# Output projections of a two-layer streaming encoder: the work on the combined tokens goes into four pieces, each placed in the engine queues behind a given split of weights

## The chip, the cores and the metric

The kernel runs on one core of a Trainium2 chip. The metric is the device time of one execution in microseconds; the median of several executions is compared. The engines go by their names in the profile: PE is TensorE (matrix products), PEld its weight loads, DVE is VectorE, ACT is ScalarE, POOL is GpSimd and SP is SyncE, which here only issues transfers.

## What is computed

The reference is one step of an encoder with two layers, on 512 prompt tokens and 8 x 16 sample tokens, 640 in all. What matters here is the last part of each layer: the outputs of three head groups are concatenated to 2048 features per token, multiplied by the output weights, and added to the residual.

```python
    y = jnp.concatenate([y_a, y_b, y_c], axis=-1) @ w_out
    return x + y, new_conv, new_k, new_v
```

All numbers are float32. The kernel keeps that precision with TensorE's faster format: it splits each operand into a rounded part and the rest, and multiplies three of the four combinations.

## The kernel before

**Layout.** Tokens are the columns: R holds 16 blocks of 128 features (rows of blocks k = 0 to 15) by 640 tokens. HL holds the split of R: blocks 0 to 15 the rounded parts, 16 to 31 the rests. The tokens are halved into TA (0 to 319) and TB (320 to 639), and the 16 feature blocks are cut into KS (0 to 3), KB (4 to 9) and KA (10 to 15).

**Splits.** `split` (line 136) makes the rounded part with one ScalarE activation (line 138) and the rest with one VectorE subtraction (line 139). It is used for tokens and for weights. Both lines therefore show in the profile for many things; the tile names tell them apart: sr is a raw block of output weights, sh its rounded part, sl its rest; th and tl are the two parts of combined tokens in tiles of their own; HL is written for the rest of the tokens.

**Output projection.** `proj` (line 740) multiplies output tiles 0 and 1 of each layer in the plain way: four weight blocks of four feature blocks, each multiplied with both token halves, three products each, so 24 matmuls of 320 columns per weight block (line 749). Tile 0 takes its weights through `wprep`, tile 1 through `s_prep` (line 773), which loads with SP into one of six sr buffers and splits into one of two sh and one of two sl buffers.

The other output tiles come in pairs through `s_pair` (line 818). It saves one of the eight products of a 2 x 2 block product over (output tile, token half) and (KA, KB), in the manner of Winograd and Strassen. a11, a21, a22 and a12 are the raw weights of the two tiles j1, j2 for KA and KB. VectorE makes the sums s1 = a21 + a22, s2 = s1 - a11, and in place a21 = a11 - a21 and a12 = a12 - s2. The products are, in the order of the code for all pairs but the last: a11 with (KA, TA) into X; a12 with (KB, TA) and a12 - s2 with (KB, TB) into z1 (`plain`); the KS columns of tile j1 and of tile j2 (`rest`; the prediction calls their weights r1 and r2); then p7, p6, p4 and p5, which multiply with the combined tokens T3, T2, T4 and T1. Each six-block product is 18 matmuls (line 810).

**Combined tokens.** `combos` (line 783) runs once per layer, after tile 1. It makes sums and differences of the token blocks in place in R (`sub`, line 778), in two groups of three blocks, and splits the results: T2, T3 and T4 into th and tl, T1 into HL over (KA, TB), which nothing else needs any more. That is eight subtractions and eight splits of 128 x 960. In layer 1 the copy y12d keeps R's (KA, TB) for the last two output tiles (line 1063); the second subtraction of a group overwrites what it reads.

**What sets the order.** The framework lays out one queue per engine before the run, from priorities, dependences and its own estimate of times; the engines then work through their queues in that order. Weights are loaded and split under `high_priority`; combos() has ordinary priority. Nothing else fixes where its work stands between the splits of weights. SP's loads are chained in program order (`load`, line 147). The residual tile of each output row is loaded by POOL into R itself (line 823), as soon as that row of R is free; a row of KB is free when T2 and T4 have been split, a row of KA when T3 and T1 have.

`tc.issue_after(ins)` makes every instruction that its block traces on ins's engine stand behind ins in that engine's queue. It is an order of issue and no wait for ins to finish.

Of the kernel before, what the change touches and what calls it, by code (L numbers as in the profile page):

```python
# [58 lines left out]
def build(nc, tc, ctx, A):  # L59
# [23 lines left out]
    def tl(shape, tag, bufs, dt=F32, pl=None):  # L83
        uid[0] += 1
        pl = pl or (cur[home[tag]] if tag in home else sb)
        return pl.tile(shape, dt, tag=tag, name=f"{tag}_{uid[0]}", bufs=bufs)
# [7 lines left out]
    def g2(shape, dt=F32):  # L94
        return tl(shape, "g2", 8, dt)
# [10 lines left out]
    def pa():  # L106
        return tl([P, 512], "a", 4, F32, ap_)

    def pz():
        return tl([P, 2, 512], "z", 2, F32, zp)  # L110
# [4 lines left out]
    R = sb.tile([P, NK, TOK], F32, tag="R", name="R")  # L115
# [8 lines left out]
    ks = Rf[:, (C0 + 3) * TOK + 288:(C0 + 3) * TOK + 288 + P]  # L124
# [8 lines left out]
    def half(t):  # L133
        return t.rearrange("p (s n) -> p s n", s=2)

    def split(raw, scale=None, hi=None, lo=None):
        if scale is None:
            a = ac.activation(hi, raw, AF.Copy)  # L138
            v = ve.tensor_tensor(out=lo, in0=raw, in1=hi.bitcast(F32), op=ALU.subtract)  # L139
        else:  # L140
            a = ac.activation(hi, raw, AF.Copy, scale=scale)
            v = ve.scalar_tensor_tensor(
                out=lo, in0=raw, scalar=scale, in1=hi.bitcast(F32), op0=ALU.mult, op1=ALU.subtract
            )
        return a.ins, v.ins
# [92 lines left out]
    def passes(a, b):  # L238
        return ((a[0], b[0]), (a[0], b[1]), (a[1], b[0]))
# [515 lines left out]
    KS, KB, KA = slice(0, 4), slice(4, 10), slice(10, 16)  # L755
    TA, TB = slice(0, HT), slice(HT, TOK)

    def s_raw(n=6):
        return tl([P, 768], "sr", 6, F32, cur["sw"])[:, :n * P]

    def s_split(raw):
        n = raw.shape[-1]
        hi = tl([P, 768], "sh", 2, F32R, cur["sw"])[:, :n]
        lo = tl([P, 768], "sl", 2, F32R, cur["sw"])[:, :n]
        split(raw, None, hi, lo)
        return hi, lo

    def s_load(src):
        raw = s_raw(src.shape[-1] // P)
        load(raw, src)  # L770
        return raw
# [5 lines left out]
    def sub(out, a, b):  # L777
        ve.tensor_tensor(out=out, in0=a, in1=b, op=ALU.subtract)

    def hl(ks, cs):  # L780
        return HL[:, ks, cs], HL[:, slice(NK + ks.start, NK + ks.stop), cs]

    def combos():
        T = {}
        tt = [
            (tl([P, 6, HT], f"th{n}", 1, F32R, cur["tt"]), tl([P, 6, HT], f"tl{n}", 1, F32R, cur["tt"]))
            for n in (2, 3, 4)
        ]
        T[2], T[3], T[4] = tt
        T[1] = hl(KA, TB)  # L790
        gs = [(slice(KA.start + g, KA.start + g + 3), slice(KB.start + g, KB.start + g + 3)) for g in (0, 3)]
        for a, b in gs:
            sub(R[:, a, TA], R[:, a, TB], R[:, a, TA])
            sub(R[:, a, TB], R[:, b, TB], R[:, a, TB])
            sub(R[:, b, TB], R[:, b, TB], R[:, a, TA])
        place = {1: (0, TA), 2: (1, TB), 3: (0, TB), 4: (1, TA)}
        for n in (3, 2, 4, 1):
            for g, ab in enumerate(gs):
                i, cs = place[n]
                if n == 4:  # L800
                    sub(R[:, ab[1], TA], R[:, ab[1], TA], R[:, ab[1], TB])
                ks = slice(3 * g, 3 * g + 3)
                split(R[:, ab[i], cs], None, T[n][0][:, ks, :], T[n][1][:, ks, :])
        return T

    def s_mm(out, w, x, start, stop):
        n = w[0].shape[-1] // P
        for k in range(n):
            for i, (a, b) in enumerate(passes(w, x)):
                pe.matmul(  # L810
                    out, a[:, k * P:(k + 1) * P], b[:, k, :], start=start and k == 0 and i == 0,
                    stop=stop and k == n - 1 and i == 2, skip_group_check=True,
                )

    def add_to(out, ps):
        ve.tensor_tensor(out=out, in0=ps, in1=out, op=ALU.add)  # L816

    def s_pair(l, j1, T, resid, early=None):
        j2 = j1 + 1
        wj = [A["w_out"][l, j1], A["w_out"][l, j2]]  # L820
        cut = [slice(ks.start * P, ks.stop * P) for ks in (KA, KB, KS)]
        for j in (j1, j2):
            gp.dma_start(R[:, j, :], resid[j])
        X, Dd = pa()[:, :HT], pa()[:, :HT]
        with tc.high_priority():
            a11 = s_load(wj[0][:, cut[0]])
            a21 = s_load(wj[1][:, cut[0]])
            a22 = s_load(wj[1][:, cut[1]])
            a12 = s_load(wj[0][:, cut[1]])
            p1 = s_split(a11)  # L830
            s1, s2 = s_raw(), s_raw()
            ve.tensor_tensor(out=s1, in0=a21, in1=a22, op=ALU.add)
            sub(s2, s1, a11)
            sub(a21, a11, a21)
        s_mm(X, p1, hl(KA, TA), True, True)
        add_to(R[:, j1, TA], X)

        z1 = z2 = None

        def rest(z, j, start, raw=None):  # L840
            with tc.high_priority():
                w = s_split(raw or s_load(wj[j - j1][:, cut[2]]))
            for s, cs in enumerate((TA, TB)):
                s_mm(z[:, s, :HT], w, hl(KS, cs), start, True)

        def plain(start):
            with tc.high_priority():
                w = s_split(a12)
            s_mm(z1[:, 0, :HT], w, hl(KB, TA), start, not start)
            with tc.high_priority():  # L850
                sub(a12, a12, s2)
                w = s_split(a12)
            s_mm(z1[:, 1, :HT], w, hl(KB, TB), start, not start)

        def into(j, z):
            add_to(half(R[:, j, :]), z[:, :, :HT])

        def mixed(raw, n, out, start, dst):
            with tc.high_priority():
                w = s_split(raw)  # L860
            s_mm(out, w, T[n], start, True)
            for j, cs in dst:
                add_to(R[:, j, cs], out)

        p6 = (s2, 2, X, False, [(j2, TA)])
        p7 = (a21, 3, Dd, True, [(j2, TB)])
        p5 = (s1, 1, X, False, [(j2, TB), (j1, TB)])
        p4 = (a22, 4, Dd, False, [(j2, TA)])
        order = (p7, p6, p4, p5)
        if early:  # L870
            for a in order:
                mixed(*a)
            with tc.high_priority():
                st = [s_load(w[:, cut[2]]) for w in wj]
            early(0)
            z1, z2 = pz(), pz()
            rest(z1, j1, True, st[0])
            rest(z2, j2, True, st[1])
            early(1)
            into(j2, z2)  # L880
            plain(False)
            early(2)
            into(j1, z1)
        else:
            z1 = pz()
            plain(True)
            rest(z1, j1, False)
            into(j1, z1)
            z2 = pz()
            rest(z2, j2, True)  # L890
            into(j2, z2)
            for a in order:
                mixed(*a)

    for l in range(L):
# [35 lines left out]
        for n, (kind, i) in enumerate(ZT):  # L931
# [9 lines left out]
            if l == 0 and 2 <= n < 10:  # L941
                for h in (n - 2, n + 6):
                    a = bscr[h:h + 1, :]
# [33 lines left out]
            elif kind in ("k", "v"):  # L977
                raw = g2([P, 512])
# [14 lines left out]
                else:  # L993
# [5 lines left out]
                    for h in range(2):  # L999
                        hi = V[h][:, :, rows2[h]]  # L1000
# [11 lines left out]
            elif kind == "q":  # L1012
                raw = zt()[:, :512]
# [4 lines left out]
                for h in range(2):  # L1018
                    q = qh([P, 512])
                    hi = q[rows2[h]]  # L1020
# [10 lines left out]
            elif kind == "cq":  # L1031
                raw = zt()[:, :512]
# [32 lines left out]
        resid = A["xT"] if l == 0 else x1d  # L1065
        done = NK if l == 0 else NK - 2
        T, W = None, []
# [29 lines left out]
        for j in list(range(2)) + list(range(2, done, 2)):  # L1097
            if j < 2:
                res = zt()
                gp.dma_start(res, resid[j])  # L1100
                ps = proj(
                    [A["w_out"][l, j][:, c * 512:(c + 1) * 512] for c in range(4)], s_prep if j else wprep
                )
                ve.tensor_tensor(out=half(R[:, j, :]), in0=ps[:, :, :HT], in1=half(res), op=ALU.add)
            else:
                s_pair(l, j, T, resid, turn if j + 2 == done else None)
            if j == 0:
                close_pool("wp")
                open_pool("tt", "right")
            if j == 1:  # L1110
                T = combos()
            for i in range(j, j + 1 if j < 2 else j + 2):
                if l == 0:
                    gp.dma_start(x1d[i], R[:, i, :])
                add_sq(i, i == 0, acc)
# [4 lines left out]
    parts = (slice(0, 384), slice(384, TOK))  # L1120
# [168 lines left out]
```

## Time and profile before

| | us |
|---|---|
| median of 3 runs (lowest, highest) | 1848.38 (1848.2, 1850.27) |
| the profiled execution | 1848.52 |
| its span, first to last instruction | 1846.7 |
| around the span | 1.8 |

The granted TensorE clock over the span is 0.997 of full speed. The first tiles of the output projection, with which the change deals, lie at about 764 to 800 us in layer 0 and 1625 to 1658 us in layer 1. The page gives busy times and shares of the span; a timeline gives instructions in order of time, start and length in us, with equal neighbours merged (the length is then that of all of them); a view by windows gives start:end, length, and for PE, PEld, DVE, ACT and POOL the busy time with the count of instructions, then the granted clock, the busy share of the DMA engines and what they moved in GB/s; the view of waits gives total, count and longest; the view of a tile gives shortest, median and longest in ns. The view of DMA issues gives the count, the size and the median time from issue to landing.

### The profile page before, as it was taken

The numbers are of one execution on the slowest core, as the hardware profiler recorded it, in microseconds if no ns is written. First come the engines' busy times: TensorE is split into PE (matmuls) and PEld (weight loads), VectorE is DVE, ScalarE is ACT, GpSimd is POOL, SyncE is SP. The second block draws the span as 40 slices with busy tenths as digits, with TensorE's granted clock in tenths as the row PEclk, the third lists the DMA queues.
The fourth block names the chain that finished last, engine by engine and source line by source line (L and its number), as shares of the span: only waits on it lengthen the run. The fifth ranks groups of instructions, "written<-read, shape, count | busy, mean of one in ns | idle before, by whom it ended". The sixth has DMA issues, their size and how long they took to land.

```text
span 1846.7 us, 32347 instructions
## 1 busy us (share of the span) xinstructions
PE 1817.5 (98%) x12612; PEld 1766.3 (96%) x12612; DVE 1257.8 (68%) x2562; ACT 786.6 (43%) x1609; POOL 160.7 (9%) x351
## 2 busy tenths in 40 slices
PE   8999999999999999999999999999999999999996
PEld 7999999999998999999999999999999899989996
DVE  7959989567555435966686999766655444676765
ACT  7832224556544334533352222555755333533331
POOL 1121210000000010100020000000000010010000
PEclk9999999999999999999999999999999999999998
DMA  8844442222222343543333332222232244452233
GB/s 281 294 122 107 103 127 76 74 63 72 84 81 76 92 158 117 167 135 112 111 98 92 81 86 77 74 68 76 67 87 81 75 132 132 140 175 76 77 113 120
DMA packets 89001, 202.30 MB, mean 110 GB/s; under 512 B 11872, under 2 KB 16912, under 8 KB 88816
## 3 DMA queue, kind: packets, MB, share of 16 engines
q1 hardware_dynamic: 68848, 139.75, 25.3%
q0 software_dynamic: 17536, 57.60, 10.1%
q10 hardware_dynamic: 2464, 2.88, 0.4%
q8 instruction: 99, 1.62, 0.4%
q14 instruction: 54, 0.44, 0.1%
HBM read 184.84 MB, written 20.33 MB: 111 GB/s over the span
## 4 chain that ended last, share of the span: by engine, by line
PE 94%; DVE 3%; DMA 1%; issue 0%; ACT 0%; DVEq 0%; ACTq 0%
PE z L749 59%; PE a L810 9%; PE z L810 9%; PE z L301 2%; PE a L278 2%; PE a L497 2%; PE a L540 2%; PE a L477 2%; PE z L1134 1%; DVE R L1167 1%; PE a L528 1%; DMA wr<-w_in 1%; PE a L636 1%; PE a L675 1%; PE a L662 1%; PE a L571 1%
## 5 line engine op out<-in xcount | busy, mean ns | idle before, releaser
L749 PE MATMUL z<-HL,wh 128*128 128x320 f32 x4992 | 973.8, 312 | 0.0
L749 PEld LDWEIGHTS z<-HL,wh 128*128 128x128 f32 x4992 | 787.8, 188 | 8.9 <-issue 5.6
L749 PE MATMUL z<-HL,wl 128*128 128x320 f32 x2496 | 584.1, 312 | 1.0 <-DVE wl L139 1.0
L749 PEld LDWEIGHTS z<-HL,wl 128*128 128x128 f32 x2496 | 419.6, 188 | 4.5 <-issue 1.6
L138 ACT ACTIVATE wh<-wr 128x512 fp32r<-128x512 f32 x316 | 198.6, 629 | 467.4 <-PE z L749 383.9
L139 DVE TENSOR_TENSOR wl<-wr,wh 128x512 fp32r<-128x512 f32 x316 | 217.7, 689 | 177.8 <-ACT wh L138 165.4
L425 DVE SCALAR_TENSOR_TENSOR R<-R,sm 128x128 f32<-128x128 f32 (+1 forms) x480 | 235.2, 550 | 0.1
L138 ACT ACTIVATE sh<-sr 128x768 fp32r<-128x768 f32 (+1 forms) x125 | 98.2, 788 | 203.3 <-PE z L810 92.4
L810 PE MATMUL z<-HL,sh 128*128 128x320 f32 x728 | 161.1, 309 | 2.9 <-ACT sh L138 2.9
L139 DVE TENSOR_TENSOR sl<-sr,sh 128x768 fp32r<-128x768 f32 (+1 forms) x125 | 110.0, 882 | 38.7 <-ACT sh L138 38.5
L810 PEld LDWEIGHTS z<-HL,sh 128*128 128x128 f32 x728 | 121.6, 188 | 4.0 <-ACT sh L138 4.0
L810 PE MATMUL z<-HL,sl 128*128 128x320 f32 x364 | 113.6, 312 | 2.3 <-DVE sl L139 2.1
L810 PEld LDWEIGHTS z<-HL,sl 128*128 128x128 f32 x364 | 68.3, 188 | 4.9 <-DVE sl L139 4.9
L810 PE MATMUL a<-th,sh 128*128 128x320 f32 x234 | 72.2, 308 | 0.0
L810 PE MATMUL a<-th,sl 128*128 128x320 f32 x234 | 72.2, 308 | 0.0
L810 PE MATMUL a<-tl,sh 128*128 128x320 f32 x234 | 72.2, 308 | 0.0
L810 PE MATMUL a<-HL,sh 128*128 128x320 f32 x312 | 68.9, 308 | 0.0
L139 DVE TENSOR_TENSOR g<-a,g 128x512 fp32r<-128x512 f32 x80 | 49.6, 634 | 27.1 <-ACT g L138 26.5
L501 DVE CUSTOM_DVE_ANT_0 g<-a,R 128x256 f32<-128x256 f32 (+1 forms) x128 | 46.4, 388 | 23.4 <-PE a L497 20.0
L138 ACT ACTIVATE g<-a 128x512 fp32r<-128x512 f32 x80 | 42.2, 552 | 42.3 <-PE a L531 29.9
L513 ACT ACTIVATE g<-g,sml 128x256 f32<-128x256 f32 (+1 forms) x128 | 59.7, 468 | 0.0
L816 DVE TENSOR_TENSOR R<-a,R 128x320 f32<-128x320 f32 x78 | 37.1, 489 | 25.3 <-PE a L810 24.8
(262 smaller groups left out, 2512.0 us busy)
## 6 DMA issues: line engine op xcount, KB each, us to landing
wr<-w_in SPq DMA_DIRECT2D x304, 256.0 KB, 2.7
sr<-w_out SPq DMA_DIRECT2D x52, 384.0 KB, 3.2
sr<-w_out SPq DMA_DIRECT2D x34, 256.0 KB, 2.6
u<-w_mv SPq DMA_DIRECT2D x16, 512.0 KB, 3.8
u<-cmkT POOLq DMA_DIRECT2D x16, 512.0 KB, 4.3
u<-cmv POOLq DMA_DIRECT2D x16, 512.0 KB, 4.4
u<-w_mk SPq DMA_DIRECT2D x14, 512.0 KB, 4.4
R<-xT SPq DMA_DIRECT2D x16, 320.0 KB, 4.1
```

Of the source, the lines that this page charges most:

```text
L138: a = ac.activation(hi, raw, AF.Copy)
L139: v = ve.tensor_tensor(out=lo, in0=raw, in1=hi.bitcast(F32), op=ALU.subtract)
L278: pe.matmul(ps[ct][:, :256], w[:, ws], mslot(l, k, lo), start=k == 0 and n == 0, stop=k == NK - 1 and n == 2,)
L301: pe.matmul(psv[:, m, :], mslot(l, k, lo)[:, ms], w, start=k == 0 and n == 0, stop=k == NK - 1 and n == 2,)
L425: ve.scalar_tensor_tensor(out=o, in0=x, scalar=w, in1=o, op0=ALU.mult, op1=ALU.add)
L477: pe.matmul(ps[:, :HT], w[:, ws], x[:, k, :], start=n == 0, stop=n == 11)
L497: pe.matmul(ps[:, j, c0:256], q[:, p * P:(p + 1) * P], kk[n][h][:, (p - 1) * P + c0:(p + 1) * P], start=n == 0, stop=n == 1,)
L501: ve.tensor_tensor_reduce(out=x[:, j, c0:], in0=ps[:, j, c0:], in1=bt[:, c0:], scale=1.0, scalar=-3.0e38, op0=ALU.add, op1=ALU.max, accum_ ...
L513: ac.activation(x, x, AF.Exp, bias=ng[:, p:p + 1], accum_out=sm_[:, p:p + 1])
L749: pe.matmul(ps[:, s, :HT], w[:, ws], HL[:, lo * NK + k, s * HT:(s + 1) * HT], start=k == 0 and n == 0, stop=k == NK - 1 and n == 2,)
L810: pe.matmul(out, a[:, k * P:(k + 1) * P], b[:, k, :], start=start and k == 0 and i == 0, stop=stop and k == n - 1 and i == 2, skip_group_c ...
L816: ve.tensor_tensor(out=out, in0=ps, in1=out, op=ALU.add)
```

## The change

`s_split` now records the two instructions of each weight split in a list, `marks`. `combos` no longer issues its work: it returns the tiles and a generator of four pieces. Piece 1 is the first six subtractions, piece 2 the splits of T3 and T2, piece 3 the two remaining subtractions and the splits of T4, piece 4 the splits of T1. `behind` issues the next piece under `issue_after` for both instructions of a marked split. Pieces 1 to 3 are placed behind the second, third and fourth weight block of tile 1 (pc1, pc2, pc3 in the prediction), piece 4 behind the split of a12 in the layer's first pair (tiles 2 and 3). The order T3, T2, T4, T1 is as it was.

```diff
--- before.py
+++ after.py
@@ -755,6 +755,8 @@
     KS, KB, KA = slice(0, 4), slice(4, 10), slice(10, 16)
     TA, TB = slice(0, HT), slice(HT, TOK)
 
+    marks = []
+
     def s_raw(n=6):
         return tl([P, 768], "sr", 6, F32, cur["sw"])[:, :n * P]
 
@@ -762,7 +764,7 @@
         n = raw.shape[-1]
         hi = tl([P, 768], "sh", 2, F32R, cur["sw"])[:, :n]
         lo = tl([P, 768], "sl", 2, F32R, cur["sw"])[:, :n]
-        split(raw, None, hi, lo)
+        marks.append(split(raw, None, hi, lo))
         return hi, lo
 
     def s_load(src):
@@ -789,19 +791,35 @@
         T[2], T[3], T[4] = tt
         T[1] = hl(KA, TB)
         gs = [(slice(KA.start + g, KA.start + g + 3), slice(KB.start + g, KB.start + g + 3)) for g in (0, 3)]
-        for a, b in gs:
-            sub(R[:, a, TA], R[:, a, TB], R[:, a, TA])
-            sub(R[:, a, TB], R[:, b, TB], R[:, a, TB])
-            sub(R[:, b, TB], R[:, b, TB], R[:, a, TA])
-        place = {1: (0, TA), 2: (1, TB), 3: (0, TB), 4: (1, TA)}
-        for n in (3, 2, 4, 1):
+
+        def parts(n, ab, g):
+            i, cs = {1: (0, TA), 2: (1, TB), 3: (0, TB), 4: (1, TA)}[n]
+            ks = slice(3 * g, 3 * g + 3)
+            split(R[:, ab[i], cs], None, T[n][0][:, ks, :], T[n][1][:, ks, :])
+
+        def work():
+            for a, b in gs:
+                sub(R[:, a, TA], R[:, a, TB], R[:, a, TA])
+                sub(R[:, a, TB], R[:, b, TB], R[:, a, TB])
+                sub(R[:, b, TB], R[:, b, TB], R[:, a, TA])
+            yield
+            for n in (3, 2):
+                for g, ab in enumerate(gs):
+                    parts(n, ab, g)
+            yield
             for g, ab in enumerate(gs):
-                i, cs = place[n]
-                if n == 4:
-                    sub(R[:, ab[1], TA], R[:, ab[1], TA], R[:, ab[1], TB])
-                ks = slice(3 * g, 3 * g + 3)
-                split(R[:, ab[i], cs], None, T[n][0][:, ks, :], T[n][1][:, ks, :])
-        return T
+                sub(R[:, ab[1], TA], R[:, ab[1], TA], R[:, ab[1], TB])
+                parts(4, ab, g)
+            yield
+            for g, ab in enumerate(gs):
+                parts(1, ab, g)
+            yield
+
+        return T, work()
+
+    def behind(work, n):
+        with tc.issue_after(marks[n][0]), tc.issue_after(marks[n][1]):
+            next(work)
 
     def s_mm(out, w, x, start, stop):
         n = w[0].shape[-1] // P
@@ -815,7 +833,7 @@
     def add_to(out, ps):
         ve.tensor_tensor(out=out, in0=ps, in1=out, op=ALU.add)
 
-    def s_pair(l, j1, T, resid, early=None):
+    def s_pair(l, j1, T, resid, early=None, later=None):
         j2 = j1 + 1
         wj = [A["w_out"][l, j1], A["w_out"][l, j2]]
         cut = [slice(ks.start * P, ks.stop * P) for ks in (KA, KB, KS)]
@@ -850,6 +868,8 @@
             with tc.high_priority():
                 sub(a12, a12, s2)
                 w = s_split(a12)
+            if later:
+                behind(later, -2)
             s_mm(z1[:, 1, :HT], w, hl(KB, TB), start, not start)
 
         def into(j, z):
@@ -1103,12 +1123,14 @@
                 )
                 ve.tensor_tensor(out=half(R[:, j, :]), in0=ps[:, :, :HT], in1=half(res), op=ALU.add)
             else:
-                s_pair(l, j, T, resid, turn if j + 2 == done else None)
+                s_pair(l, j, T, resid, turn if j + 2 == done else None, work if j == 2 else None)
             if j == 0:
                 close_pool("wp")
                 open_pool("tt", "right")
             if j == 1:
-                T = combos()
+                T, work = combos()
+                for n in (-3, -2, -1):
+                    behind(work, n)
             for i in range(j, j + 1 if j < 2 else j + 2):
                 if l == 0:
                     gp.dma_start(x1d[i], R[:, i, :])
```

## The prediction

> **What bounds the kernel now.** I read the page first, for the engine that bounds; then TensorE's timeline around the first tiles of the output projection in both layers, for its waits; then the queues of VectorE and ScalarE there, for what stood ahead of the late weights; then the DMA view, for what comes next.
>
> From the page, span and busy shares:
>
> ```profile
> span 1846.7 us, 32347 instructions
> PE 1817.5 (98%) x12612; PEld 1766.3 (96%) x12612; DVE 1257.8 (68%) x2562; ACT 786.6 (43%) x1609; POOL 160.7 (9%) x351
> ```
>
> TensorE (PE) is idle for 29 us in all. The change adds or removes no matmul, so all it can win is idle time of PE. PE's timeline, layer 0 and then layer 1 (start, length, instruction; in brackets the idle time before it and who ended it):
>
> ```profile
> 774.74 0.56 PE L749 MATMUL z<-HL,sl 128*128 128x320 f32 x2 [1.66 <-DVE sl L139]
> ...
> 777.78 0.75 PE L749 MATMUL z<-HL,sh 128*128 128x320 f32 x4
> ...
> 778.66 0.75 PE L749 MATMUL z<-HL,sh 128*128 128x320 f32 x4
> ...
> 794.01 0.56 PE L810 MATMUL z<-HL,sh 128*128 128x320 f32 x2 [0.68 <-ACT sh L138]
> 794.73 0.42 PE L810 MATMUL z<-HL,sl 128*128 128x320 f32 x1 [0.17 <-DVE sl L139]
> ```
>
> ```profile
> 1634.60 0.56 PE L749 MATMUL z<-HL,sl 128*128 128x320 f32 x2 [0.42 <-DVE sl L139]
> 1642.25 0.56 PE L810 MATMUL z<-HL,sh 128*128 128x320 f32 x2 [0.35 <-ACT sh L138]
> 1646.69 0.41 PE L810 MATMUL z<-HL,sl 128*128 128x320 f32 x1 [1.53 <-DVE sl L139]
> 1650.71 0.56 PE L810 MATMUL z<-HL,sh 128*128 128x320 f32 x2 [1.41 <-ACT sh L138]
> 1651.71 0.41 PE L810 MATMUL z<-HL,sl 128*128 128x320 f32 x1 [0.44 <-DVE sl L139]
> ```
>
> Layer 0 waits 1.66 + 0.68 + 0.17 = 2.51 us, layer 1 0.42 + 0.35 + 1.53 + 1.41 + 0.44 = 4.15 us: **6.66 us** together, always for a split of weights (sh is its rounded part, made by ScalarE, sl the rest, made by VectorE). The eleven later pairs of tiles run with no combination work beside them, and there PE waits almost never: the view of PE's waits has one row for 800 to 1590 us and none for 1655 to 1790:
>
> ```profile
> PE z L810 <- ACT sh L138: 0.5, 1, 0.5
> ```
>
> So the waits belong to what is special here: combos(). Why the weights were late shows in VectorE's (DVE) and ScalarE's (ACT) timelines of layer 0. I call the four weight blocks of tile 1 pc0 to pc3.
>
> ```profile
> 754.11 1.29 DVE L139 TENSOR_TENSOR sl<-sr,sh 128x512 fp32r<-128x512 f32 x2
> 755.31 1.16 DVE L778 TENSOR_TENSOR R<-R 128x960 f32<-128x960 f32 x1
> ...
> 770.79 3.29 DVE L139 TENSOR_TENSOR tl<-R,th 128x960 fp32r<-128x960 f32 x3
> 774.00 0.69 DVE L139 TENSOR_TENSOR sl<-sr,sh 128x512 fp32r<-128x512 f32 x1
> ...
> 783.11 1.15 DVE L139 TENSOR_TENSOR HL<-R,HL 128x960 fp32r<-128x960 f32 x1
> 784.18 0.95 DVE L778 TENSOR_TENSOR sr<-sr,sr 128x768 f32<-128x768 f32 x1
> ```
>
> ```profile
> 769.16 0.62 ACT L138 ACTIVATE sh<-sr 128x512 fp32r<-128x512 f32 x1
> ```
>
> ScalarE had pc2's rounded part ready at 769.78, but VectorE made pc2's rest only at 774.00: a subtraction and three splits of combined tokens (tl) were queued ahead. That is the 1.66 us. Layer 1 has the same crowding, with a later start:
>
> ```profile
> 1625.63 2.23 DVE L778 TENSOR_TENSOR R<-R 128x960 f32<-128x960 f32 x2 [3.17 <-DMA y12d<-R]
> ...
> 1645.67 0.96 DVE L139 TENSOR_TENSOR sl<-sr,sh 128x768 fp32r<-128x768 f32 x1
> ...
> 1648.73 0.97 DVE L778 TENSOR_TENSOR sr<-sr,sr 128x768 f32<-128x768 f32 x1
> ```
>
> ```profile
> 1649.82 1.36 ACT L138 ACTIVATE sh<-sr 128x768 fp32r<-128x768 f32 x2 [3.28 <-DVE sr L778]
> ```
>
> There VectorE stands still for 3.17 us until the copy y12d has read R, and the backlog then delays a12's rest (1645.67) and the subtraction for a12−s2 (1648.73), for which ScalarE waits 3.28 us and PE after it.
>
> **The change, part by part.** No instruction is added or dropped: eight subtractions and eight splits per layer stay, by these rows of the tile view about 1.0 us on ScalarE and 1.16 us on VectorE each (three of them back to back took 3.29 us, so 1.07 us of VectorE's time).
>
> ```profile
> L138 ACT ACTIVATE th<-R x12: 990/1006/1011, 760.3 to 1636.7; 128x960 fp32r<-128x960 f32 x12
> L139 DVE TENSOR_TENSOR tl<-R,th x12: 1152/1158/1165, 767.6 to 1640.2; 128x960 fp32r<-128x960 f32 x12
> ```
>
> *Piece 1*, six subtractions behind pc1's split: they already start behind it (755.31 after 754.11). Nothing moves: 0 us. In layer 1 they still wait for y12d.
>
> *Piece 2*, four splits (T3, T2) behind pc2's split. pc2's rest now comes first: in layer 0 at about 769.8 instead of 774.0, where PE wants it at 774.74 − 1.66 = 773.1. The 1.66 us go. In layer 1, four subtractions and tile 0's addition (5 us from 1625.63) end at about 1630.7, pc2's rest at 1631.4; PE wants it at 1634.2. The 0.42 us go.
>
> *Piece 3*, two subtractions and two splits (T4) behind pc3; *piece 4*, two splits (T1) behind a12's split in the first pair. What they stood ahead of moves forward: a12 and a12−s2. PE's pitch sets the demand: from 777.78 to 778.66 six matmuls, 0.147 us each, so 24 matmuls (one pc, or one block of the plain columns) last 3.52 us and 18 (a six-block product) 2.64 us. Counted from the end of pc0's matmuls, PE wants pc3's rest at about 7.6, a11's at 10.8, a12's at 13.5, a12−s2's at 16.1, the two plain blocks' (r1, r2) at 18.8 and 22.3, T3 at 25.5, T4 at 30.8. VectorE's work over this stretch is 8 splits and 2 subtractions of combined tokens (10 × 1.07 = 10.7), six weight splits (about 4.4), four weight sums (3.5) and three additions (about 1.9): 20.5 us, of which only some 8 us are wanted by 16.1. The cover for the rest: VectorE is nearly idle from 788 to 794 us, while r1 is multiplied,
>
> ```profile
> 788.00:794.00 6.00, 5.33 (x37) 5.06 (x35) 0.05 (x2) 0.68 (x2) 0.00 (x0) 1.00 0.63 223
> ```
>
> 0.05 us busy in six (the third figure with its count). T3 to T1 finish there, before T3 is wanted. If that cover were gone they would be late by what is left, 1.07 us a split.
>
> *The added order* costs nothing by itself, since it is issue order on one engine. Behind a delayed piece on VectorE stand only the tile additions and the square sums, which nobody in this stretch waits for; on ScalarE only the next weights' rounding. What it can cost: each urgent instruction may find one piece in progress (1.0 us on ScalarE, 1.07 on VectorE), and one that depends on its forerunner loses its place to a piece, as 784.18 behind 783.11 shows. The tightest chain is a12 → a12−s2: rounding, rest, subtraction, rounding, rest, 4.75 us with nothing between, against 5.57 us allowed after a11's product begins. With three pieces in between it is 7.9, 2.3 us late. So 0 to 2.3 us a layer, 0 to 0.6 for r1. In layer 0 before, this chain had one piece and two other instructions in it, and PE's timeline has no bracket there; more work now stands beside it, so I take 0.6 us a layer, near the low end: **1.2 us**.
>
> *Transfers that move with it.* The pieces free rows of R, and POOL then loads later residual tiles into them (12 of 320 KB in layer 0, 10 in layer 1). r2's weights come beside these, by the DMA view of single issues (layer 0's r2, issued at 787.16; then r1, at 779.99):
>
> ```profile
> sr<-w_out SPq DMA_DIRECT2D x1, 256.0 KB, 6.1
> ```
>
> ```profile
> sr<-w_out SPq DMA_DIRECT2D x1, 256.0 KB, 3.1
> ```
>
> ```profile
> 784.56 1.59 POOL L823 DMA_DIRECT2D R<-xT  x3 [1.07 <-DVE HL L139]
> ```
>
> r2 took 6.1 us beside loads such as these, r1 3.1 us clear of them: this, not VectorE, made the 0.85 us at 794. After the change r2 is asked for when a12−s2 is split, at about 15.5 on the clock above, and the six loads freed by T1 come after it; only three to six freed by T4 are beside it. It may take 3.1 to 6.1 us; 5.4 are allowed. I take the 0.85 us as gone and no new wait; the other end is 0.7 a layer.
>
> [...]
>
> The **sum**: −6.66 + 1.2 = −5.5 us, on the profiled execution's 1848.52 us (span 1846.7 and 1.8 around it) 1843.0; from the median of 1848.38 it is **1842.9**. What is saved stays saved: from 800 to 1590 us PE does not wait for anything that is fixed in time, and after layer 1 PE still sets the end.
>
> **The rivals.**
>
> *Half of it comes back.* The weights lose to pieces nearby instead of to a block of them, 2 to 2.9 us a layer (upper ends above). Against it: the slack of each step but one is over 1.5 us. For it: VectorE is full in layer 1, 4.00 of 4.00 us:
>
> ```profile
> 1642.00:1646.00 4.00, 2.91 (x18) 2.64 (x18) 4.00 (x6) 1.30 (x3) 2.43 (x6) 1.00 0.90 296
> ```
>
> −6.66 + 4.7 = −2.0: 1846.4.
>
> *Nothing changes that counts.* issue_after sets only a lower bound; the rest of the queue order is laid out from estimated times, and other work may slip ahead of the weights. Against it: nothing of size is left but these pieces. 1848.4.
>
> *Slower: the residual loads bunch ahead of r2.* If pieces 3 and 4 end together before r2's load is issued, all loads stand ahead of it. At the rate of this window, 369 GB/s,
>
> ```profile
> 1650.00:1654.00 4.00, 2.85 (x17) 2.59 (x18) 1.56 (x2) 1.18 (x2) 0.00 (x0) 1.00 0.96 369
> ```
>
> 320 KB take 0.89 us, twelve 10.7 and ten 8.9; r2 itself adds at least 2 of its 3.1. Against 5.4 allowed that is 7.3 and 5.5 us late: 12.8 − 5.5 = +7.3, 1855.7. The gain is used up at 2.75 us a layer, from seven loads ahead of r2 in each (2 + 7 × 0.89 − 5.4). For it: r2's 6.1 us. Against it: piece 4 stands behind a12's split, and its last split ends after a12−s2's.
>
> **How the numbers follow.** Forecast 0.60 (its own range 1841.3 to 1844.6), half back 0.20, nothing 0.10, slower 0.08, more than all waits 0.02. A measurement here can tell about 0.2%, 3.7 us, from no change. Faster by more: the forecast and a little of the half case, 0.62; within: 0.30; slower: 0.08. The range 1841.3 to 1848.0 leaves out the slow rival, what is above none, and the lowest tail.
>
> **What would show it.** pc2's rest right after its rounding, before any tl, in both layers, and no bracket of 1.66 us at PE's pc2; in layer 1 no wait over 1 us from 1634 to 1652; T1's splits behind a12's; a12−s2 late by under 1 us; r2 landed in under 5.4 us. I am wrong if PE's idle time in the two stretches stays above 3 us, if it shows up at r2 or at p7 to p5, or if tiles far from here change.

## The result, and the profile after

| | before | after |
|---|---|---|
| median (lowest, highest) of 6 runs each, us | 1847.49 (1845.25, 1850.27) | 1853.56 (1852.92, 1856.07) |
| ratio after / before, 95% interval | | 1.0033 [1.0023, 1.0043] |
| the profiled execution / its span, us | 1848.52 / 1846.7 | 1853.72 / 1851.9 |

The change made the kernel slower by 0.33%, some 6 us. The prediction was 1842.9 us, and its range ended at 1848.0. The page after (span, busy time of the engines, share, instructions):

```profile
span 1851.9 us, 32343 instructions
PE 1821.2 (98%) x12612; PEld 1769.8 (96%) x12612; DVE 1257.9 (68%) x2562; ACT 785.9 (42%) x1609; POOL 160.7 (9%) x351
```

PE executes the same 12612 matmuls, but they took 3.7 us longer (1821.2 against 1817.5), and PE also stood still longer. So two things have to be found. The waits first: PE's timeline after, layer 0 and layer 1, those rows that have a bracket. Lines below 755 are as before; the matmuls of `s_pair` are L828 now (L810 before), `sub` is L780 (L778), the addition of a pair's output L834 (L816).

```profile
783.88 0.42 PE L828 MATMUL z<-HL,sl 128*128 128x320 f32 x1 [1.70 <-DVE sl L139]
...
788.98 0.66 PE L828 MATMUL z<-HL,sh 128*128 128x320 f32 x2 [2.48 <-ACT sh L138]
789.98 0.63 PE L828 MATMUL z<-HL,sl 128*128 128x320 f32 x1 [0.33 <-DVE sl L139]
...
798.12 0.42 PE L828 MATMUL z<-HL,sl 128*128 128x320 f32 x1 [0.17 <-DVE sl L139]
...
1649.26 0.42 PE L828 MATMUL z<-HL,sl 128*128 128x320 f32 x1 [1.70 <-DVE sl L139]
...
1654.36 0.56 PE L828 MATMUL z<-HL,sh 128*128 128x320 f32 x2 [2.48 <-ACT sh L138]
1655.35 0.41 PE L828 MATMUL z<-HL,sl 128*128 128x320 f32 x1 [0.43 <-DVE sl L139]
```

No row of line 749 (tile 1) has a bracket any more: the 1.66 and 0.42 us of pc2 are gone, as forecast. In their place both layers wait 1.70 us for a12's rest and 2.48 + 0.33 or 0.43 us for a12−s2. Together 4.68 + 4.61 = 9.29 us, against 6.66 before.

Why they are late is read in the queues of VectorE and ScalarE, layer 0:

```profile
768.78 0.69 DVE L139 TENSOR_TENSOR sl<-sr,sh 128x512 fp32r<-128x512 f32 x1 [2.82 <-ACT sh L138]
...
780.01 1.16 DVE L139 TENSOR_TENSOR tl<-R,th 128x960 fp32r<-128x960 f32 x1
781.08 0.82 DVE L1124 TENSOR_TENSOR R<-z,zt 128x640 f32<-128x640 f32 x1
781.81 1.16 DVE L139 TENSOR_TENSOR tl<-R,th 128x960 fp32r<-128x960 f32 x1
782.87 0.96 DVE L139 TENSOR_TENSOR sl<-sr,sh 128x768 fp32r<-128x768 f32 x1
783.74 1.16 DVE L139 TENSOR_TENSOR HL<-R,HL 128x960 fp32r<-128x960 f32 x1
784.81 0.49 DVE L834 TENSOR_TENSOR R<-a,R 128x320 f32<-128x320 f32 x1
785.21 1.16 DVE L139 TENSOR_TENSOR HL<-R,HL 128x960 fp32r<-128x960 f32 x1
786.28 0.83 DVE L255 TENSOR_TENSOR w<-w,w 128x640 f32<-128x640 f32 x1
787.01 0.96 DVE L780 TENSOR_TENSOR sr<-sr,sr 128x768 f32<-128x768 f32 x1
```

```profile
768.12 0.63 ACT L138 ACTIVATE sh<-sr 128x512 fp32r<-128x512 f32 x1 [1.39 <-PE z L749]
...
779.31 0.84 ACT L138 ACTIVATE sh<-sr 128x768 fp32r<-128x768 f32 x1
...
788.09 1.36 ACT L138 ACTIVATE sh<-sr 128x768 fp32r<-128x768 f32 x2 [5.42 <-DVE sr L780]
```

Three places matter here. pc2's rest (768.78) follows its rounding (768.12) directly. a12's rounding was done at 780.15, but its rest began at 782.87, because piece 3's two T4 splits (tl) and a tile addition stood ahead: 2.86 us from 780.01. And piece 4's two T1 splits (HL) stand behind a12's split, as written, but that is **directly ahead of the subtraction a12−s2** (787.01): they, an addition and a square sum fill 783.74 to 787.01, 3.27 us. ScalarE waits 5.42 us for that subtraction, and PE after it. Layer 1 has the same order.

Second, the matmuls that took longer. Windows after (start:end, length, busy time and count of PE, PEld, DVE, ACT, POOL, granted clock, DMA share, GB/s), placed around the 2.48 us of both layers:

```profile
786.00:789.30 3.30, 0.82 (x6) 0.54 (x4) 2.31 (x4) 1.21 (x2) 1.74 (x4) 1.00 0.97 372
789.30:792.70 3.40, 3.07 (x12) 2.72 (x11) 1.22 (x2) 0.15 (x1) 0.65 (x2) 0.50 1.02 407
792.70:796.00 3.30, 3.30 (x24) 3.30 (x23) 0.00 (x0) 0.00 (x0) 0.00 (x0) 1.00 1.04 393
1653.00:1656.20 3.20, 1.41 (x8) 1.15 (x8) 1.91 (x3) 1.36 (x2) 0.32 (x1) 1.00 0.99 376
1656.30:1659.70 3.40, 3.40 (x15) 3.40 (x14) 0.00 (x0) 0.00 (x0) 0.00 (x0) 0.50 1.01 397
```

After each long wait **the granted clock falls to 0.50 for 3.4 us** and is 1.00 again after it: 12 and 15 matmuls where the next stretch has 24. In the trace the clock's stretches at one half are 789.29 to 792.71 and 1656.28 to 1659.69, 3.41 us each, half of which is lost: 1.7 us a fall, 3.41 in all. Before, no stretch of the projection was below 1.00.

Waits +2.63, clock +3.41, all other waits of PE, those of 0.15 us and more, −0.7 (10.8 against 11.5): +5.3 us, against 5.2 us between the spans, 1851.9 − 1846.7.

### The profile page after: what moved, and what is told of

Its sections match the earlier page's. It is cut to its first block, busy times and chain, and to the rows that moved or that the text cites. A ratio compares the mean times of both kernels' runs of the same rounds, so it can differ in the third digit from the quotient of the medians.

```text
span 1851.9 us, 32343 instructions
## 1 busy us (share of the span) xinstructions
PE 1821.2 (98%) x12612; PEld 1769.8 (96%) x12612; DVE 1257.9 (68%) x2562; ACT 785.9 (42%) x1609; POOL 160.7 (9%) x351
## 4 chain that ended last, share of the span: by engine, by line
PE 95%; DVE 3%; DMA 1%; issue 0%; ACT 0%; DVEq 0%; ACTq 0%; POOLq 0%
PE z L749 59%; PE a L828 9%; PE z L828 9%; PE a L278 3%; PE z L301 2%; PE a L497 2%; PE a L540 2%; PE a L477 2%; PE z L1156 1%; DVE R L1189 1%; PE a L528 1%; DMA wr<-w_in 1%; PE a L636 1%; PE a L675 1%; PE a L662 1%; PE a L571 1%
## 5 line engine op out<-in xcount | busy, mean ns | idle before, releaser
L828 PE MATMUL z<-HL,sh 128*128 128x320 f32 x728 | 163.4, 313 | 5.5 <-ACT sh L138 5.5
L828 PEld LDWEIGHTS z<-HL,sh 128*128 128x128 f32 x728 | 123.7, 191 | 6.6 <-ACT sh L138 6.6
L828 PE MATMUL z<-HL,sl 128*128 128x320 f32 x364 | 115.0, 316 | 4.3 <-DVE sl L139 4.3
L828 PEld LDWEIGHTS z<-HL,sl 128*128 128x128 f32 x364 | 69.5, 191 | 7.3 <-DVE sl L139 7.3
L828 PE MATMUL a<-th,sh 128*128 128x320 f32 x234 | 72.2, 309 | 0.0
L828 PE MATMUL a<-tl,sh 128*128 128x320 f32 x234 | 72.2, 309 | 0.0
L828 PE MATMUL a<-th,sl 128*128 128x320 f32 x234 | 72.2, 308 | 0.0
L828 PE MATMUL a<-HL,sh 128*128 128x320 f32 x312 | 69.1, 309 | 0.1
L834 DVE TENSOR_TENSOR R<-a,R 128x320 f32<-128x320 f32 x78 | 37.1, 489 | 25.4 <-PE a L828 24.8
```

Of the source, the lines that this page charges most:

```text
L828: pe.matmul(out, a[:, k * P:(k + 1) * P], b[:, k, :], start=start and k == 0 and i == 0, stop=stop and k == n - 1 and i == 2, skip_group_c ...
```

## The experiments

**Theory A**: what is issued directly ahead of the next urgent link costs its own length; piece 4 between a12's split and the subtraction, and piece 3's T4 splits ahead of a12's rest, make the waits, and a long wait costs a clock fall on top. **Rival B**: the late combination work frees the rows of R late and at once, and POOL's loads of residuals delay weights. All times stand against runs of the kernel before on the same chip; each diff is against the changed kernel unless it says otherwise.

**1. Piece 4 one split later, behind a12−s2's.**

```diff
-                behind(later, -2)
+                behind(later, -1)
```

> Theory A (queue place and clock): in the changed kernel both T1 splits stand ahead of the subtraction a12-s2 on VectorE, PE waits 2.48 us there, and the clock then falls to half for 3.4 us (1.7 us lost), in each layer. With T1 behind the split of a12-s2 instead, that wait falls under 0.6 us and the clock stays whole in both layers; the wait of 1.70 us for a12's rest, made by T4's splits, stays. 2 x (1.9 to 2.5 + 1.7) less than the changed kernel's 1853.6: 1845 to 1846.5, ratio to before 0.999 to 1.000. Rival B (the residual loads): the lost time comes from POOL's twelve loads bunched ahead of r2's weights; later T1 splits bring them nearer to r2, so no gain, 1853 or more. Rival C (VectorE is simply too full in this stretch, whatever the order): the wait only moves, to a12-s2's rest or to r1, 1851 to 1854.

Measured: 1846.43 us (1845.68 to 1847.35), ratio to before 0.9993 [0.9984, 1.0002]: 7.1 us below the changed kernel's median (7.4 by the two ratios to before), from one index. Layer 0, VectorE and then PE:

```profile
783.18 0.95 DVE L139 TENSOR_TENSOR sl<-sr,sh 128x768 fp32r<-128x768 f32 x1
...
785.18 0.95 DVE L780 TENSOR_TENSOR sr<-sr,sr 128x768 f32<-128x768 f32 x1
```

```profile
784.18 0.41 PE L828 MATMUL z<-HL,sl 128*128 128x320 f32 x1 [1.70 <-DVE sl L139]
...
787.14 0.56 PE L828 MATMUL z<-HL,sh 128*128 128x320 f32 x2 [0.34 <-ACT sh L138]
788.13 0.41 PE L828 MATMUL z<-HL,sl 128*128 128x320 f32 x1 [0.44 <-DVE sl L139]
```

The subtraction stands 2.00 us after the start of a12's rest instead of 4.14, and its wait goes from 2.48 to 0.34: 2.14 us less in both, the length of the two T1 splits (1.07 us each). The 1.70 us of a12's rest stays, as it should, and no fall of the clock is left. Waits −4.3 and clock −3.4 make −7.7, and the spans differ by 7.3.

**2. Pieces 1 and 2 placed, T4's and T1's work in the framework's order** (T3 and T2 behind pc2's split).

```diff
-                s_pair(l, j, T, resid, turn if j + 2 == done else None, work if j == 2 else None)
+                s_pair(l, j, T, resid, turn if j + 2 == done else None, None)
...
-                for n in (-3, -2, -1):
+                for n in (-3, -2):
                     behind(work, n)
+                for _ in work:
+                    pass
```

> T3 and T2 placed behind pc2's split as in the change, T4 and T1 without a place. Theory A: pc2's waits of before (1.66 and 0.42 us) are gone, since nothing of combos can stand ahead of pc2's rest; by the queue order one T1 split stands between a12's rest and the subtraction in layer 1, as before, so a12's waits there stay between 1 and 3.5 us; no fall of the clock. 1845 to 1847, ratio 0.998 to 1.000. Rival B: the loads are freed at about the times of before, so the time of before, 1847 to 1848. Rival C: 1847 or more, the wait moves.

Measured: 1846.8 us, 0.9996 [0.9987, 1.0005], no change. In the profiled execution (1848.27 us) layer 1's waits were 4.32 us and had one fall of the clock, which the expectation had excluded. VectorE and PE there:

```profile
1634.63 3.28 DVE L139 TENSOR_TENSOR tl<-R,th 128x960 fp32r<-128x960 f32 x3
1637.83 0.68 DVE L139 TENSOR_TENSOR sl<-sr,sh 128x512 fp32r<-128x512 f32 x1
```

```profile
1638.57 0.56 PE L749 MATMUL z<-HL,sl 128*128 128x320 f32 x2 [1.97 <-DVE sl L139]
```

The wait of pc2 was only handed on to pc3's rest, 1.97 us here and 0.93 in layer 0. Five splits of combined tokens now stand between the two rests, T3's, T2's and one of T4's; the first row shows the last three. Moving a block behind one urgent split puts it ahead of the next.

**3. Only T4 and T1 placed**: pieces 1 and 2 in the framework's order, pieces 3 and 4 as in the change.

```diff
-                for n in (-3, -2, -1):
-                    behind(work, n)
+                next(work)
+                next(work)
+                behind(work, -1)
```

> Only T4 (behind pc3) and T1 (behind a12) placed, T3 and T2 free as before. Theory A: the whole loss comes from these two, so a12 waits about 1.7 us, a12-s2 2 to 3 us, and the clock falls once per layer as in the changed kernel; pc2's waits of before come back on top (up to 1.7 and 0.4 us). 1853 to 1856, ratio 1.003 to 1.005. Rival C: nearer to before, 1848 to 1851, since T3 and T2 relieve VectorE early again.

Measured: 1849.89 us (1849.27 to 1851.04), 1.0009 [1.0000, 1.0017]: less than A expected, and in the range of its rival C. pc2's waits did not come back, since in layer 0 T3's and T2's splits run early again (VectorE, from 765.63 to 769.98). a12−s2 waited 1.78 us in layer 0 and 2.49 in layer 1, so piece 4 does its harm here too; a12's rest waited 1.13 in layer 1 only. And the clock fell in one layer, not the one with the longer wait. Layer 0, right behind the 1.78 us:

```profile
787.30:790.70 3.40, 3.34 (x12) 3.34 (x13) 0.61 (x2) 0.00 (x0) 0.13 (x1) 0.50 1.03 417
```

So a fall isn't decided by the length of one wait alone; experiments 7 and 8 are about that.

**4. T4 behind a12−s2's split, T1 later still, behind the last split of the pair's plain columns.**

```diff
-                behind(later, -2)
+                behind(later, -1)
...
+            if later:
+                behind(later, -1)
...
-                for n in (-3, -2, -1):
+                for n in (-3, -2):
```

> T3 and T2 behind pc2's split, T4 behind the split of a12-s2, T1 behind r1's split. Theory A: no combined token stands ahead of any of pc3, a11, a12, a12-s2; PE's waits in the two stretches fall from 6.66 us of before to under 2 us and the clock stays whole: 1842 to 1844, ratio 0.997 to 0.999. Rival B: all twelve residual loads are now freed around r1 and r2, r2 comes 3 us late or more in each layer: 1848 to 1854. Rival C: the waits move to T3 (p7) or T4 (p4), which are needed 25 and 31 us after pc0, or to r1 and r2; 1847 or more.

Measured: 1848.88 us (1846.7 to 1850.92), 1.0008 [0.9999, 1.0017], where A expected a gain; the time is in rival B's range. The profiled execution is the fastest of the eleven, 1846.7 us, so the trace shows where the waits arise, but not what the median has above it. Nothing waits at a12 or a12−s2 any more, but PE waits 0.49 us for the rounded weights of p7 and then at the pair's end. POOL, VectorE and PE of layer 0:

```profile
788.86 4.24 POOL L841 DMA_DIRECT2D R<-xT  x8 [7.71 <-DVE HL L139]
```

```profile
802.67 0.96 DVE L850 TENSOR_TENSOR sr<-sr,sr 128x768 f32<-128x768 f32 x1 [2.67 <-DMA sr<-w_out]
```

```profile
804.17 0.54 PE L828 MATMUL a<-HL,sh 128*128 128x320 f32 x2 [0.62 <-DVE R L834]
...
805.81 0.42 PE L828 MATMUL a<-HL,sl 128*128 128x320 f32 x1 [1.10 <-DVE sl L139]
```

Here B shows itself. Eight residual loads are issued from 788.86, behind T1's splits (HL). The weights of the next pair, asked for at 794.00, land at 802.54, and VectorE stands 2.67 us in front of the sum s1, for which nothing is in a hurry. But its queue is in order, and the addition that frees a product (L834) and the next split stand behind it. B is real, at a place later than the prediction's: the next pair's first weights, not r2.

**5. As 1, with T4's work halved**: both T4 subtractions and the first T4 split behind pc3's split, the second T4 split together with T1 behind a12−s2's.

```diff
-            for g, ab in enumerate(gs):
-                sub(R[:, ab[1], TA], R[:, ab[1], TA], R[:, ab[1], TB])
-                parts(4, ab, g)
+            for a, b in gs:
+                sub(R[:, b, TA], R[:, b, TA], R[:, b, TB])
+            parts(4, gs[0], 0)
             yield
+            parts(4, gs[1], 1)
...
-                behind(later, -2)
+                behind(later, -1)
```

> Like the run with T1 behind a12-s2's split, but the T4 work is cut: both T4 subtractions and the first T4 split stand behind pc3's split, the second T4 split goes with T1 behind a12-s2's split. Theory A (what stands directly ahead of the next urgent weights costs its own length): a12's rest loses one T4 split ahead of it, PE's wait for it falls from 1.70 to 0.7 us or less in each layer, a12-s2's stays under 0.8, no clock fall: about 1.5 us a layer less than that run's 2.5, time 1843.5 to 1845.5. Rival B (the later splits free residual rows all at once, and POOL's loads then delay weights): the wait goes to r2 or to the next pair, 1 us or more there, time 1846.5 or more.

```profile
783.87 0.42 PE L829 MATMUL z<-HL,sl 128*128 128x320 f32 x1 [0.63 <-DVE sl L139]
```

One T4 split less ahead of a12's rest, and its wait goes from 1.70 to 0.63 in both layers: 1.07 us, one split exactly. That reads the mechanism. The time doesn't follow: 1846.94 us, 0.9994 [0.9986, 1.0003], as in experiment 1 and in rival B's range. In layer 0, the plain columns (0.43) and a later product (0.83 at 807.40) wait instead, in layer 1 the plain columns (0.31). The 0.83 us are B again. Nine residual loads are issued from 789.15, and VectorE then stands in front of the next pair's sum s1, with the split that PE wants behind it:

```profile
804.25 0.96 DVE L851 TENSOR_TENSOR sr<-sr,sr 128x768 f32<-128x768 f32 x1 [1.52 <-DMA sr<-w_out]
```

In experiment 1 VectorE does not wait at this place. In layer 0 of experiments 6 (first run) and 9 it does, 1.39 and 1.46 us, and PE waits 0.70 and 0.77 us after it.

**6. T1 alone moved**: pieces 1 to 3 in the framework's order, T1 behind a12−s2's split.

```diff
-                behind(later, -2)
+                behind(later, -1)
...
-                for n in (-3, -2, -1):
-                    behind(work, n)
+                for _ in range(3):
+                    next(work)
```

> Pieces 1 to 3 are left to the order of before (not placed), T1 alone stands behind the split of a12-s2. Theory A: pc2's waits of before are back (about 1.66 and 0.4 to 2 us), a12's rest and a12-s2 wait for at most one split (under 1.2 us each), so 2.5 to 4.5 us of waits in the two layers together against 6.7 before, no clock fall, 1844.5 to 1847. Rival: the waits of before do not come from T1 at all, and they stay near 6.7 us: 1847 to 1849.

Measured: 1844.51 us, 0.9981 [0.9972, 0.9990]; a second time, beside experiment 9:

> The same kernel as the run with T1 alone behind a12-s2's split, on the same chip as its rival arrangement: 1843.5 to 1845.5 again if its 0.9981 of before is no accident; 1846 or more if it is.

1844.25 us, 0.9987 [0.9978, 0.9996]. pc2's 1.67 us are there as before, and of the waits behind it at most 0.7 a piece: 4.4 us in the two layers together (2.36 + 2.00), 3.7 the second time. T1's work between the weights of the first pair was worth taking away; the three pieces in front were not what the change needed.

**7 and 8. What a wait costs the clock.** Experiment 1 with three (7) or six (8) multiplications of a12 by 1.0 on VectorE between its subtraction and its split, in all pairs but the first of each layer. The output isn't changed, work is added.

```diff
                 sub(a12, a12, s2)
+                for _ in range(0 if later else 3):
+                    ve.tensor_scalar(out=a12, in0=a12, scalar1=1.0, scalar2=None, op0=ALU.mult)
                 w = s_split(a12)
```

> The run with T1 behind a12-s2's split, with three multiplications of a12 by 1.0 on VectorE between its subtraction and its split in each of the eleven later pairs (work added, nothing left out). It lengthens PE's wait for a12-s2 there by a step per pair; one costs somewhere from 0.45 to 0.95 us, and 0.8 us of slack is taken off first, so 0.5 to 2 us of wait a pair. Clock theory: the granted clock falls to half for 3.41 us (1.7 us lost) wherever PE was idle for more than about 1.8 us within one 3.41 us stretch of a fixed grid; here in none or a few pairs, time 1846.4 + waits + 1.7 per fall. Rival: a wait costs its length only, 1846.4 + waits, with the clock at full speed between.

> The same with six multiplications: 2 to 4.9 us of wait a pair. Clock theory: most or all of the eleven pairs show a fall to half for 3.41 us or a multiple, about 11 x 1.7 = 19 us on top of the waits' own sum; a wait of over 1.9 us that lies astride a border of the grid, with less than 1.8 us on each side, shows none. Rival: waits cost their length only.

Measured: 1882.24 and 1909.57 us (two executions each). One multiplication took 0.56 us. Three of them made nine waits of the same length, 1.93 us, at the same instruction, of which PE's timeline shows two:

```profile
905.68 0.56 PE L828 MATMUL z<-HL,sh 128*128 128x320 f32 x2 [1.93 <-ACT sh L138]
...
934.11 0.56 PE L828 MATMUL z<-HL,sh 128*128 128x320 f32 x2 [1.93 <-ACT sh L138]
```

and the windows behind them differ:

```profile
905.80:909.20 3.40, 2.97 (x19) 2.71 (x20) 1.43 (x2) 0.35 (x1) 0.00 (x0) 1.00 0.39 122
935.90:939.20 3.30, 3.30 (x14) 3.30 (x13) 0.00 (x0) 0.27 (x1) 0.00 (x0) 0.50 0.58 199
```

Six of the nine waits were followed by a fall, three were not; the expectation had named none or a few pairs. The falls of experiment 7 start at 816.35, 847.07, 877.79, 935.81, 987.01, 1731.12 and 1789.14 us (the one at 987.01 follows a tenth pair's waits of 1.21 and 0.43 us): their distances are multiples of 3.413 us (30.72 is nine of them, 853.33, from 877.79 to 1731.12, is 250). So these changes of the clock lie on a grid of 3.41 us, and those of the changed kernel do too: from 789.29 to 1656.28 us is 254 times 3.413. PE's idle time can be cut at the lines of that grid. In the changed kernel, from 20 to 1815 us, the pieces with 2.48 and 1.92 us (from 785.88 and 1652.87 us) are followed by a fall, and the next, with 1.70 us (from 1646.04), is not. Before the change the fullest piece had 1.54 us, and there is no fall. In experiment 3 the piece with a fall behind it has about 2.15 us: the 1.78 and most of the 0.44 us that follow. Layer 1's 2.49 us there lie across a line, with about 1.74 and 0.75 us on its sides, and stay without a fall. The three waits of experiment 7 that were spared lie across a line: two with 1.34 and 1.02, 1.33 and 1.04 us on its sides, each counted with the 0.43 us that follows it, and one with 1.67 on the fuller side. In experiment 8 ten waits of 3.71 to 4.04 us were each followed by a fall, three of them over two stretches of the grid. So in these runs the fall, and its 1.7 us, went with **the idle time inside one stretch of the grid** rather than with the length of one wait: 1.92 us in one stretch had it behind them, 2.49 us across two had not. There is no sharp limit: the fall at 987.01 follows 1.21 + 0.43 = 1.64 us, and the changed kernel's 1.70 us have none behind them.

The totals agree: against experiment 1 PE waits 23.0 us more in 7 and PE's busy time is 14.0 longer, 37.0 of the span's 37.5; in 8 it is 40.6 and 22.0, 62.6 of 63.0. By the rival, that a wait costs its length only, the second term would not be there. The traces have 7 and 13 stretches at half clock, which lose 11.9 and 22.2 us; the other 2.1 us of busy time in 7 stay unexplained.

**9. All four places again, filled earlier**: T3's splits move up behind pc1's split with the six subtractions, T2's splits and both T4 subtractions stand behind pc2's, one T4 split behind pc3's, the other T4 split and T1 behind a12−s2's.

```diff
+            for g, ab in enumerate(gs):
+                parts(3, ab, g)
             yield
-            for n in (3, 2):
-                for g, ab in enumerate(gs):
-                    parts(n, ab, g)
-            yield
+            for g, ab in enumerate(gs):
+                parts(2, ab, g)
             for g, ab in enumerate(gs):
                 sub(R[:, ab[1], TA], R[:, ab[1], TA], R[:, ab[1], TB])
-                parts(4, ab, g)
             yield
+            parts(4, gs[0], 0)
+            yield
+            parts(4, gs[1], 1)
...
-                behind(later, -2)
+                behind(later, -1)
```

> All four places again, but earlier fillings: T3's two splits move up behind pc1's split with the six subtractions (VectorE stood still for 2.8 us ahead of pc2's rest), T2's splits and both T4 subtractions behind pc2's, one T4 split behind pc3's, the other T4 split and T1 behind a12-s2's. Theory A: pc2's wait stays gone, a12's 1.70 goes to under 0.5, a12-s2's to 0.8 or less, a11's rest may come up to 0.8 us late behind the T4 split; 1 to 2 us of waits a layer, no clock fall, 1843 to 1845.5, at or below the run with T1 alone moved. Rival B: what is filled in earlier makes pc2's or pc3's weights late again (1 us or more there), 1846 or more.

Measured: **1843.41 us** (1842.33 to 1844.68), 0.9977 [0.9969, 0.9986], the fastest of all, 10 us below the changed kernel's median. It is 0.8 us below experiment 6 on the same chip, with intervals that overlap. Layer 0, VectorE, and then what PE still waits for in this stretch of both layers:

```profile
765.08 2.22 DVE L139 TENSOR_TENSOR tl<-R,th 128x960 fp32r<-128x960 f32 x2
767.98 0.69 DVE L139 TENSOR_TENSOR sl<-sr,sh 128x512 fp32r<-128x512 f32 x1 [0.69 <-ACT sh L138]
```

```profile
778.73 0.56 PE L830 MATMUL z<-HL,sh 128*128 128x320 f32 x2 [0.35 <-ACT sh L138]
787.20 0.56 PE L830 MATMUL z<-HL,sh 128*128 128x320 f32 x2 [0.28 <-ACT sh L138]
...
1636.40 0.57 PE L749 MATMUL z<-HL,sl 128*128 128x320 f32 x2 [1.03 <-DVE sl L139]
1645.26 0.41 PE L830 MATMUL z<-HL,sl 128*128 128x320 f32 x1 [0.37 <-DVE sl L139]
1648.53 0.56 PE L830 MATMUL z<-HL,sh 128*128 128x320 f32 x2 [0.36 <-ACT sh L138]
```

In the changed kernel VectorE stood still for 2.82 us ahead of pc2's rest (the bracket at 768.78 above) and then had no idle time until the subtraction ended at 787.97. T3's two splits fit into that hole: the idle time is 0.69 us now, pc2's rest is not later for it, and a12's rest is on time. The 1.03 us are pc3's rest in layer 1, behind T2's splits and both T4 subtractions: there the expectation's rival B holds, though the time is A's. The waits shown, with 0.77 us at 803.19, are 3.16 us in the two layers together.

## Why the prediction was wrong, step by step

*Piece 1 at nothing, and piece 2's two waits* were right: pc2's rest follows its rounding, and line 749 has no bracket. What the second step left out is where the four splits went: ahead of pc3's rest. In the changed kernel nothing waits there; in experiment 2, with one T4 split more, pc3's rest is 0.93 and 1.97 us late.

*"What they stood ahead of moves forward: a12 and a12−s2"* is the step that failed, for both pieces. It was the wrong way round: piece 3 is directly ahead of a12's rest, piece 4 directly ahead of the subtraction.

- a12's rest had no term in the sum: the prediction compared due times with the work left in total (20.5 us, "only some 8 us are wanted by 16.1") and found slack over 1.5 us. The sum of work says nothing about its order. The two T4 splits and a tile addition, 2.86 us, came first; 1.70 us a layer, and 0.63 with one split less (experiment 5).
- The chain a12 → a12−s2 was bounded by 0 and 2.3 us and taken at 0.6. By the prediction's own figures, 4.75 us plus the 3.27 that stand between split and subtraction are 8.02 against 5.57 allowed: 2.45 late; measured 2.48 us, and 0.33 or 0.43 behind it. That the two agree so closely is partly luck: the chain also stood 2.72 us ahead of a12's rest (780.15 to 782.87), and PE, which waited 1.70 us there, wanted a12−s2 that much later. Experiment 1 is the cleaner measure, 2.14 us for the two T1 splits. The bound was about right, the value taken from the wrong end. The reason given was that layer 0 before had one piece in the chain and no bracket; the change put in two.

With both, 1.2 us of residual waits became 9.29 (8.1 of the miss).

*The clock* was no term at all (3.41 of the miss). Each wait of the profile before stayed without a fall, the fullest grid stretch there having 1.54 us, so that profile did not show the price. The other waits of PE gave 0.7 us back (10.8 against 11.5, above). 8.1 + 3.4 − 0.7 = 10.8 us, against the 10.7 between −5.5 and the span's +5.2.

*The transfers.* In layer 0 r2 took 6.7 us (after, DMA issues: count, size, median us to landing), not under 5.4; in layer 1 it took 4.8. Layer 0:

```profile
sr<-w_out SPq DMA_DIRECT2D x1, 256.0 KB, 6.7
```

PE waited only 0.17 us for it, since PE itself was late. So the 0.85 us were nearly gone, though for another reason, and the slow rival (loads ahead of r2) isn't what made the kernel slower; that it exists, at the next pair's first weights, is seen in experiments 4, 5, 6 and 9.

*The rivals.* "Half of it comes back" named the mechanism ("the weights lose to pieces nearby") and priced it at 2 to 2.9 us a layer; it was 4.6 to 4.7, and with the clock 6.3 to 6.4.

*The signs named beforehand*: pc2 right; "T1's splits behind a12's" right, and just there the harm; no wait over 1 us from 1634 to 1652 in layer 1 wrong (1.70), a12−s2 late by under 1 us wrong (2.48), r2 under 5.4 wrong in layer 0. "I am wrong if PE's idle time in the two stretches stays above 3 us" came true, with 9.29. Beyond r2's 0.17 us the tiles further on wait as before: 0.49 us once, at 958.19 (954.80 before).

What stays open: why the framework's layout let T1's splits pass the subtraction, which is traced at high priority, was not tried. It is open too why experiment 5, with 0.6 us less of waits from 764 to 812 and from 1625 to 1672 us than experiment 1 (4.38 against 4.95), is not faster. In the profiled executions it is 0.75 us behind experiment 1 already at 729 us, ahead of these tiles, so that two single profiles cannot settle it.

## What to carry to other kernels

"Behind X" fixes only one side: name what stands next behind X on the same engine, and whether it is a link of the urgent chain; here the difference between `-2` and `-1` was 7.1 us. Fill an engine's idle time *ahead of* the first urgent item before moving work behind it, and draw the queue in order against due times, not its sum. When PE is the bound, price a long wait with what the clock takes on top: in the changed kernel 1.7 us behind 1.92 and behind 2.48 us of idle time in a stretch of 3.41, nothing behind 1.70.

## What the runs showed of the hardware

That the granted clock falls behind PE's idle time was not expected: in the changed kernel 1.92 and 2.48 us of it in a stretch of 3.41 were followed by 3.41 us at 0.50 and 1.70 us were not, in experiment 7 already 1.64 us were, and there the same 1.93 us cost 1.7 us more or nothing, by where it lay on the grid. The position of the grid isn't that of the kernel's start: in the profile before, the clock first came to 1.00 at 9.59 us, in the changed kernel's at 11.05, and the later changes of both lie on the grid that runs from there (789.29 is 228 times 3.413 us behind 11.05). So one profile of a kernel with such waits shows one throw: those of experiments 2 and 3 have a fall in one layer each, the changed kernel's in both.

Weights requested beside a batch of residual loads took 6.7 us (r2, layer 0, 256 KB) after the change, and 3.0 in experiment 1, where the batch starts 1.4 us after the request; clear of such loads 256 KB took 2.5 us (after the change, issued at 811.83). The next pair's weights (384 KB) took 8.5 us in experiment 4, from 794.00 to 802.54; in experiment 1 the four loads of 384 KB issued from 784 to 800 us had a median of 7.0.
